# A hybrid decoder block in fp32 on one core: part of the FFN's input as seven half-block products, a wide projection, and a written-out order

## The chip, the cores and the metric

One core of a Trainium2 chip runs the kernel. Its engines work in parallel, each through its own instructions in order: TensorE (PE, matrix products; its weight loads are listed as PEld), VectorE (DVE), ScalarE (ACT), GpSimd (POOL) and SyncE (SP), which here only starts transfers. Transfers are carried out by 16 DMA engines. The metric is the device time of one execution in microseconds; lower is better.

## The reference

One decoder layer on 256 tokens of 1024 channels, all in float32, cut to what matters here:

```
proj = x @ w_in                     # 1024 x 9216: hq hf hi hg | mq mk mv | gate logits
y_a  = hgrn2_mixer(hq, hf, hi) normed, times silu(hg)
y_b  = moba_attention(rope(mq), rope(mk), mv)
g_a, g_b = split(sigmoid(gate_logits + b_gate))
mixed = (g_a * (y_a @ w_branch_a) + g_b * (y_b @ w_branch_b)) @ w_out
x = layer_norm(ALPHA * x + mixed, ln1_w, ln1_b)
h_gate, h_up = split(x @ w_ffn_in)  # 1024 x 2*2816
y = (silu(h_gate) * h_up) @ w_ffn_down
out = layer_norm(ALPHA * x + y, ln2_w, ln2_b)
```

## The kernel before

**Products in split precision.** Each float32 operand is split into a high part, rounded to the format that TensorE takes at full rate, and a low part, the remainder: `split` (L209) casts on ACT and subtracts on DVE. A product is then three: high times high, high times low, low times high. Weights are split on the chip too. `stage` (L217) loads one block of 1 MB into a `raw` buffer (three of them, four once `state["four"]` is set), casts it to `wh` on ACT (L236) and subtracts to `wl` on DVE (L238); there are four `wh` and four `wl` buffers. The blocks come in one fixed list from `plan` (L80), 89 of them. `fetch` (L258) takes the next finished block and first stages more until a given number is ready beyond it (LOOKAHEAD, 3); `prefetch` stages a given number.

**Three ways to arrange a product of 256 columns of weights with 256 tokens.** `feat_pair` (L298): 48 matmuls of 256 columns. `wide_pair` (L306): the high and the low part of the activations lie side by side in a `Pair`, and one matmul of 512 columns multiplies both with `wh`, a second one of 256 columns takes `wl`: 32 matmuls; the two halves of the PSUM bank are added afterwards, with a copy on ACT and an addition on DVE for each 128 columns (`wide_sum`, L321). The third is for 1024 columns of weights: `quad_stage` (L607) makes a 2 x 2 block product (two token halves, two column blocks of 512, two halves of the 1024 input channels) with seven half-block products instead of eight. Each is one `block_product` (L328): 12 matmuls of 512 columns. For that it needs differences of activations (`differences`, L335) and sums of weight blocks.

**Sums of weights.** The sums are made by transfers, not by an engine: `sum_weights` (L247) copies one weight block in DRAM into a tile `u` and adds others onto it with an accumulating transfer, both issued from POOL's queue. Eight transfers (`SUMS`, L46) make the four sums of one product; a blocked pair needs them before its weights are staged. When each is issued is written out: `SUMS_WITH` (L44) names for each of the 32 sums the load behind which it goes. A DVE copy of one element (the tick, L253) and a POOL operation (the mark, L254) tie it there. Sums keep their order in POOL's queue, and a sum that reads or adds to another's result waits there until that one has landed.

**Stages.** Input projection and the scan; gates; value and MoBA products with rope; `za` = y_a @ w_branch_a (wide); `zb` = y_b @ w_branch_b (L769, `feat_pair`); output projection `wo` (L890 to L898) with the first layer norm (`norm1`), whose result is transposed and split into `x1p` (L845); "early" FFN blocks j = 0 and 2, a token half at a time (`FfnEarly`, L855); the FFN loop (L956) over j = 4 to 20 in steps of two: a wide pair `fg` and a wide pair `fu`, silu, product, split into `ah`, `al`; the differences for the down projection (`mixed_a`, L926); the down projection, two 2 x 2 blocks of seven products each (`quad_product`, L986) and six rows of plain products (`rows_pass`); the second layer norm and the store.

**What sets the order.** Outside of `tc.manual_schedule` a planner orders each engine's instructions by a simulated timeline. Inside it, the named engines keep program order. Before the change the first projection, `wo` with the early FFN blocks, and parts of the very end are in such a block; zb, the FFN loop and nearly all of the down projection are the planner's. The residual `xr` (L828) and the norms' weights `wb` (L779, L780) are loaded from POOL's queue.

## Time and profile before

| what | value |
|---|---|
| device time, median of 3 runs | 492.39 us (492.26 to 494.57) |
| span of the profiled execution, first to last instruction | 491.3 us |
| the profiled execution's own time beside the span | not listed; the median stands 1.1 us above the span |
| PE busy | 482.9 us, 98% |
| DVE busy | 396.2 us, 81% |
| ACT busy | 315.6 us, 64% |
| POOL busy | 66.0 us, 13% |
| data moved | 137.79 MB, 280 GB/s |
| zb, starts on PE | from about 259 us |
| wo and early FFN | 283 to 328 us |
| FFN loop | 328 to 429 us |
| down projection and end | 429 to 491 us |

Lines like L315 are lines of the kernel. A row of the timeline gives the start, the length, the engine, line and operation, what it writes and reads, and how often in a row; the time that the engine idled ahead of it stands in brackets. Matmuls overlap: one of 512 columns is listed with 0.39 us, though the next starts sooner. A row of the windows gives for one stretch the busy time of each engine with its count of instructions, the clock that TensorE was granted, the share of time that the DMA engines were busy, and the rate. A row of groups gives the count, the busy time in all, the mean of one in ns, and the idle time ahead.

### The profile page before, as it was taken

How to read it: one execution, taken by the hardware profiler on the slowest of the kernel's cores; microseconds unless marked ns; L12 is line 12 of the kernel's file. 1: busy time of each engine (PE TensorE's matmuls, PEld its weight loads, DVE VectorE, ACT ScalarE, POOL GpSimd, SP SyncE). 2: the span in 40 equal slices, each digit the busy share in tenths (PEclk: the TensorE clock that was granted, in tenths of full speed). 3: DMA queues.
4: the chain of work that ended last, by engine and by line, in shares of the span. 5: the costliest groups of instructions: out<-in, count | busy, mean ns of one | idle time of the engine just before them, and what ended most of it. 6: DMA issues, size and time to landing. Idle time of an engine off the chain costs nothing.

```text
span 491.3 us, 7536 instructions
## 1 busy us (share of the span) xinstructions
PE 482.9 (98%) x2980; PEld 434.0 (88%) x2980; DVE 396.2 (81%) x490; ACT 315.6 (64%) x446; POOL 66.0 (13%) x89
## 2 busy tenths in 40 slices
PE   9999999999999999999999999999999999999994
PEld 9999888888888999999989988888888888898883
DVE  4888899999879869999773999555886779589947
ACT  6797677655879869789762555444565656587700
POOL 2305150530000010010010000001213010000001
PEclk9999999999999999999999999999999999999998
DMA  8879899999996988669776466049999999999702
GB/s 315 371 263 448 273 294 339 316 356 300 343 330 248 318 300 301 229 228 338 255 268 248 177 257 233 18 176 407 286 307 354 317 310 308 297 361 387 257 0 85
DMA packets 25106, 137.79 MB, mean 280 GB/s; under 512 B 2416, under 2 KB 2544, under 8 KB 13424
## 3 DMA queue, kind: packets, MB, share of 16 engines
q1 hardware_dynamic: 15264, 100.63, 53.2%
q0 software_dynamic: 9808, 36.70, 29.0%
q8 instruction: 23, 0.38, 0.3%
q14 instruction: 11, 0.09, 0.0%
HBM read 136.27 MB, written 34.60 MB: 348 GB/s over the span
## 4 chain that ended last, share of the span: by engine, by line
PE 95%; DVE 2%; DMA 2%; issue 0%; ACT 0%; DVEq 0%
PE fu L315 7%; PE fg L315 7%; PE fg L316 3%; PE fu L316 3%; PE gb L315 3%; PE za L315 3%; PE wd L999 2%; PE wd L1000 2%; PE wd L1001 2%; DMA raw<-in_wts_dram 2%; PE sc L514 2%; PE hf L383 2%; PE ga L315 2%; PE hf L384 2%; PE mk L355 2%; PE zb L355 2%
## 5 line engine op out<-in xcount | busy, mean ns | idle before, releaser
L238 DVE TENSOR_TENSOR wl<-raw,wh 128x2048 fp32r<-128x2048 f32 x89 | 203.0, 2289 | 54.0 <-ACT wh L236 53.5
L236 ACT CAST wh<-raw 128x2048 fp32r<-128x2048 f32 x89 | 169.8, 1916 | 73.9 <-PE fg L315 17.6
L315 PE MATMUL fg<-x1p,wh 128*128 128x512 f32 x144 | 50.5, 394 | 0.0
L315 PE MATMUL fu<-x1p,wh 128*128 128x512 f32 x144 | 50.4, 394 | 0.0
L254 POOL TENSOR_TENSOR mark<-ticks 128x1 f32<-128x1 f32 x32 | 24.4, 762 | 180.8 <-DVE ticks L253 159.9
L316 PE MATMUL fg<-x1p,wl 128*128 128x256 f32 x144 | 40.0, 277 | 0.0
L316 PE MATMUL fu<-x1p,wl 128*128 128x256 f32 x144 | 39.9, 277 | 0.0
L315 PEld LDWEIGHTS fu<-x1p,wh 128*128 128x128 f32 x144 | 27.0, 187 | 6.2
L315 PEld LDWEIGHTS fg<-x1p,wh 128*128 128x128 f32 x144 | 27.0, 187 | 6.1
L316 PEld LDWEIGHTS fg<-x1p,wl 128*128 128x128 f32 x144 | 27.0, 188 | 0.1
L316 PEld LDWEIGHTS fu<-x1p,wl 128*128 128x128 f32 x144 | 27.0, 188 | 0.0
L315 PE MATMUL za<-yP,wh 128*128 128x512 f32 x64 | 23.6, 407 | 0.0
L315 PE MATMUL gb<-xP,wh 128*128 128x512 f32 x64 | 22.7, 397 | 0.0
L315 PE MATMUL ga<-xP,wh 128*128 128x512 f32 x64 | 22.6, 396 | 0.0
L256 POOL DMA_DIRECT2D u<-in_wts_dram x24 | 19.7, 827 | 9.7 <-DMA u<-in_wts_dram 7.3
L353 PE MATMUL mq<-xP,wh 128*128 128x256 f32 x64 | 18.6, 291 | 0.0
L354 PE MATMUL mk<-xP,wh 128*128 128x256 f32 x64 | 18.4, 288 | 0.0
L353 PE MATMUL mk<-xP,wh 128*128 128x256 f32 x64 | 18.3, 285 | 0.0
L316 PE MATMUL za<-yP,wl 128*128 128x256 f32 x64 | 18.3, 285 | 0.0
L355 PE MATMUL mq<-xP,wl 128*128 128x256 f32 x64 | 18.2, 284 | 0.0
L355 PE MATMUL mk<-xP,wl 128*128 128x256 f32 x64 | 18.1, 283 | 0.0
L353 PE MATMUL hq<-xP,wh 128*128 128x256 f32 x64 | 18.1, 283 | 0.0
(338 smaller groups left out, 1388.3 us busy)
## 6 DMA issues: line engine op xcount, KB each, us to landing
raw<-in_wts_dram SPq DMA_DIRECT2D x73, 1024.0 KB, 6.3
raw<-u SPq DMA_DIRECT2D x16, 1024.0 KB, 6.7
u<-in_wts_dram POOLq DMA_DIRECT2D x8, 1024.0 KB, 20.5
u<-u POOLq DMA_DIRECT2D x8, 1024.0 KB, 18.2
first<-in_xw_dram SPq DMA_DIRECT2D x6, 640.0 KB, 9.3
xr<-in_x_dram POOLq DMA_DIRECT2D x1, 1024.0 KB, 5.2
wb<-in_ln_w_dram POOLq DMA_DIRECT2D x2, 512.0 KB, 6.6
wb<-in_ln_b_dram POOLq DMA_DIRECT2D x2, 512.0 KB, 7.9
```

The costliest lines, as they stand in the source:

```text
L236: nc.scalar.copy(h[:, ks, :], raw[:, ks, :])
L238: eng.tensor_sub(l[:, ks, :], raw[:, ks, :], r32(h[:, ks, :]))
L254: tc.keep_in_program_order(nc.gpsimd.tensor_tensor(mark, tick, tick, op=ALU.add))
L256: tc.keep_in_program_order(nc.gpsimd.dma_start(source(dst), source(src), **more))
L315: nc.tensor.matmul(ps, wh[:, k, wcol], a.both(k), start=(k == 0), stop=False)
L316: nc.tensor.matmul(ps[:, 0, :], wl[:, k, wcol], a[0, k, slice(0, T)], start=False, stop=(k == KC - 1))
L353: nc.tensor.matmul(ps, wh[:, k, wcol], ah[:, kk, :], start=(kk == 0), stop=False)
L354: nc.tensor.matmul(ps, wh[:, k, wcol], al[:, kk, :], start=False, stop=False)
L355: nc.tensor.matmul(ps, wl[:, k, wcol], ah[:, kk, :], start=False, stop=(kk == KC - 1))
L383: nc.tensor.matmul(pss[f], wh[:, wcol], xTh[:, k, :], start=(k == 0), stop=False)
L384: nc.tensor.matmul(pss[f], wh[:, wcol], xTl[:, k, :], start=False, stop=False)
L514: nc.tensor.matmul(ps[:, a, :], KL[:, h, :], later(Qt, n, h, 1), start=True, stop=True)
```

## The change

Three things, and what they need:

1. The FFN's column blocks j = 4 and 6 (512 gate and 512 up columns: `fg4`, `fu4`, `fg6`, `fu6`, four wide pairs, four loads) leave the loop. They become one `quad_stage` with gate and up columns as its two column blocks: seven products `q0` to `q6`, seven loads, four of them sums of weights. It needs the differences of x1, so a float32 copy of the transposed x1 is kept (`x1Tr`), and eight more sums. Its result lies by tokens, so it is turned by eight transposes (`turned`). `SUMS_WITH` now has 40 entries: the new group's eight go behind loads 29 to 37, and the down projection's sixteen behind loads 38 to 55 (before: four behind 38 to 41, twelve behind 56 to 67, in the FFN loop).
2. zb is made with `wide_pair`; its attention result is a `Pair` now.
3. zb's pairs 1 to 3, the FFN loop and the down projection go into `manual_schedule` for PE, DVE and ACT, with `FFN_ORDER` as the list of steps: `g` and `u` pairs, `q` products, `t` transposes, `m` differences, `s` splits. Each step stages one later load. The splits of most FFN results subtract on POOL instead of DVE. `xr` and `wb1` stand before zb in the program instead of behind it.

```diff
-SUMS_WITH = (2, 3, 4, 5, 6, 7, 8, 10, 9, 11, 12, 13, 14, 15, 16, 26,
-             38, 39, 40, 41, 56, 57, 58, 59, 60, 61, 62, 63, 64, 65, 66, 67)
+SUMS_WITH = (2, 3, 4, 5, 6, 7, 8, 10, 9, 11, 12, 13, 14, 15, 16, 26, 29, 31, 33, 34, 35, 36, 36, 37, 38, 39, 40, 41, 42, 43, 44, 45, 46, 47, 50, 51, 52, 53, 54, 55)
+GROUP = (EARLY * P, FF + EARLY * P)
+FFN_ORDER = [(i[0], int(i[1:])) for i in "g8 u8 g10 q0 u10 q1 g12 q2 u12 q3 g14 q4 u14 q5 m1 g16 t0 q6 u16 g18 t1 m0 s16 u18 s18 g20 u20 s20".split()]
...
-    for j in range(EARLY, NF, 2):
-        add("w_ffn_in", 0, 8, j * P, 256)
-        add("w_ffn_in", 0, 8, FF + j * P, 256)
+    for kind, j in FFN_ORDER:
+        if kind not in "guq":
+            continue
+        if kind == "q":
+            steps.append((quarter("w_ffn_in", 0, GROUP, GATE_PRODUCTS[j]), KQ // 2, False))
+        else:
+            add("w_ffn_in", 0, 8, (FF if kind == "u" else 0) + j * P, 256)
...
-    ybh = slot("ybh", F32R).rearrange("p (h t) -> p h t", h=H)
-    ybl = slot("ybl", F32R).rearrange("p (h t) -> p h t", h=H)
+    yb = Pair("yb")
+    ybh, ybl = Part(yb, 0), Part(yb, 1)
...
+    def zb_pair(j, ordered):
+        z = kept[:, j % 2, :].rearrange("p (f t) -> p f t", f=2)
+        more = stage() if ordered else iter(())
+        wide_sum(wide_pair(f"zb{j}", mm, "mm", yb, 0 if ordered else LOOKAHEAD), [z[:, f, :] for f in range(2)])
+        next(more, None)
+        cs = slice(2 * j, 2 * j + 2)
+        nc.vector.tensor_mul(gb[:, cs, :], z, gb[:, cs, :])
+        nc.vector.tensor_add(ga[:, cs, :], ga[:, cs, :], gb[:, cs, :])
+        next(more, None)
+        split(mTh[:, cs, :], mTl[:, cs, :], ga[:, cs, :])
+        list(more)
...
+        for ks, ps in pss:
+            nc.scalar.copy(x1Tr[:, ks, ts], ps)
...
     with tc.manual_schedule(engines={ET.PE, ET.DVE, ET.Activation}):
+        for j in range(1, 4):
+            zb_pair(j, True)
         tiles = [(2 * q,) + fetch(0) for q in range(4)]
...
+        mixing = differences(lambda t, k: x1Tr[:, k:k + 4, t * P:(t + 1) * P], xs, x1Sh, x1Sl)
         e[1][0].product(0)
+        next(mixing)
         e[1][0].product(1)
         e[0][0].transpose()
         e[0][1].transpose()
+        more = stage()
+        next(more)
         e[1][0].silu()
+        list(more)
+        more = stage()
+        next(more)
         e[1][1].product(0)
         e[1][1].product(1)
...
+        e[1][1].silu()
+        list(more)
+        next(mixing)
+        prefetch(1)
...
+    def late_half(kind, j):
+        i, p, tag = (0, mm, "mm") if kind == "g" and j >= KW else (kind == "u", aux, "aux")
+        pss = wide_pair(f"f{kind}{j}", p, tag, x1p, 0)
+        s = room[:, 2 * i + j // 2 % 2, :, :]
+        for f, ps in enumerate(pss):
+            nc.scalar.copy(s[:, f, :], ps[:, 1, :])
+        more = stage()
+        next(more, None)
+        for f, ps in enumerate(pss):
+            nc.vector.tensor_add(s[:, f, :], ps[:, 0, :], s[:, f, :])
+        both[kind] = s
+        if i == 0:
+            nc.scalar.activation(s, s, AF.Silu)
+            list(more)
+        else:
+            ...
+            nc.vector.tensor_mul(a, both["g"], both["u"])
+            list(more)
+            made[j] = a
+            if j < KW:
+                split_a(j)
...
+        split(ah[i][:, k:k + 2, ts], al[i][:, k:k + 2, ts], made[j][:, :, ts], nc.gpsimd if j >= KQ else nc.vector)
...
+        return quad_stage("gu", Part(x1p, 0), Part(x1p, 1), x1Sh, x1Sl, gu, final, kept[:, 0, :], True, 0)
+
+    def turned(t):
+        ts = slice(t * P, (t + 1) * P)
+        pt = aux.tile([P, 4, P], F32, tag="aux", name=f"gut{t}")
+        for a in range(4):
+            nc.tensor.transpose(pt[:, a, :], gu[:, t, a * P:(a + 1) * P], ident)
+        js = slice(EARLY, EARLY + 4)
+        nc.scalar.copy(araw[0][:, js, ts], pt)
+        split(ah[0][:, js, ts], al[0][:, js, ts], araw[0][:, js, ts], nc.gpsimd)
+
+    products = group()
+    with tc.manual_schedule(engines={ET.PE, ET.DVE, ET.Activation}):
+        for n, (kind, j) in enumerate(FFN_ORDER):
+            state["four"] = n > 0
+            if kind == "q":
+                next(products, None)
+                list(stage())
+            elif kind == "t":
+                turned(j)
+            elif kind == "m":
+                list(mixed_a(j))
+            elif kind == "s":
+                split_a(j)
+            else:
+                late_half(kind, j)
+            if n in (0, 1):
+                e[1][n - 0].transpose()
...
             wh, wl = fetch(0)
...
+            if i == 0:
+                list(stage())
...
+    with tc.manual_schedule(engines={ET.PE, ET.DVE, ET.Activation}):
+        quad_product(0, pss[0][:1])
+        nc.scalar.copy(p, pss[0][0][0])
+        prefetch(1)
+        ...
+        tiles = [(k,) + fetch(0) for k in range(KW, NF, 2)]
+        rows_pass(pss[0], lhs, 0, tiles, NF, True)
+        layer_norm("n2", 0, pss[0], x1[:, 0, :], wb2, x1[:, 0, :], store=out[0:P, :], made=(1,))
         rows_pass(pss[1], lhs, 1, tiles, NF, True)
```

More of the change, by code (lines that the diff above doesn't have):

```diff
@@ L725, in moba_head @@
         nc.tensor.matmul(po[:, P:T], mv[:, 1, hd], pT, start=False, stop=True)
-        split(ybh[:, h, :], ybl[:, h, :], po)
+        split(ybh[:, h, slice(0, T)], ybl[:, h, slice(0, T)], po)
         yield
@@ L766, in hybrid_layer_kernel @@
     gate = pool("gate", 1)
-    mTh = slot("mTh", F32R).rearrange("p (k t) -> p k t", k=KC)
-    mTl = slot("mTl", F32R).rearrange("p (k t) -> p k t", k=KC)
-    for j in range(4):
-        ps = feat_pair(f"zb{j}", ybh, ybl)
-        cs = slice(2 * j, 2 * j + 2)
-        nc.vector.tensor_mul(gb[:, cs, :], ps, gb[:, cs, :])
-        nc.vector.tensor_add(ga[:, cs, :], ga[:, cs, :], gb[:, cs, :])
-        split(mTh[:, cs, :], mTl[:, cs, :], ga[:, cs, :])
     def bcast(name, w, b):
@@ L781, in bcast @@
         return t
+    xr = slot("xr").rearrange("p (t d) -> p t d", t=NT)
+    nc.gpsimd.dma_start(xr, x.rearrange("(t p) d -> p t d", p=P))
+    wb1 = bcast("wb1", ln1_w, ln1_b)
+    mTh = slot("mTh", F32R).rearrange("p (k t) -> p k t", k=KC)
+    mTl = slot("mTl", F32R).rearrange("p (k t) -> p k t", k=KC)
+    kept = gate.tile([P, 2, 512], F32, tag="kept", name="kept")
+    def zb_pair(j, ordered):
[9 more added lines that the diff above has]
+        list(more)
+    for j in range(1):
+        zb_pair(j, False)
     def rows_pass(parts, lhs, t, tiles, ktot, onto=False):
@@ L846, in norm1_transpose @@
         ts = slice(t * P, (t + 1) * P)
+        pss = []
         for g in range(2):
@@ L896, in hybrid_layer_kernel @@
             rows_pass(pss[1], lhs, 1, tiles[q:q + 1], KC)
-            if q < 2:
+            if q == 0:
                 prefetch(1)
-        early = [ready.pop(0) for _ in range(4)]
-        e = [[FfnEarly(t, 2 * i, *early[2 * i:2 * i + 2]) for i in range(2)] for t in range(NT)]
+        more = stage()
+        next(more)
+        early = [ready.pop(0) for _ in range(3)]
+        e = [[None, None], [None, None]]
+        e[0][0] = FfnEarly(0, 0, *early[:2])
         e[0][0].product(0)
@@ L903, in hybrid_layer_kernel @@
         norm1(1)
+        list(more)
+        early.append(ready.pop(0))
+        e[0][1] = FfnEarly(0, 2, *early[2:])
+        e[1] = [FfnEarly(1, 2 * i, *early[2 * i:2 * i + 2]) for i in range(2)]
         e[0][0].silu()
@@ L1030, in hybrid_layer_kernel @@
         rows_pass(pss[1], lhs, 1, tiles, NF, True)
-    with tc.manual_schedule(engines={ET.DVE}):
         layer_norm("n2", 1, pss[1], x1[:, 1, :], wb2, x1[:, 1, :], store=out[P:T, :], made=(0, 1))
```

153 lines of the change are left out of this document (79 added, 74 removed).

## The prediction

> **What bounds the kernel now.** I read the page's first two parts, then what TensorE (PE) waited for, then the windows of the stages that the change touches, and last single rows of the timeline. The page:
>
> ```profile
> span 491.3 us, 7536 instructions
> PE 482.9 (98%) x2980; PEld 434.0 (88%) x2980; DVE 396.2 (81%) x490; ACT 315.6 (64%) x446; POOL 66.0 (13%) x89
> PEclk9999999999999999999999999999999999999998
> ```
>
> PE's waits, both of them, and its last matmul:
>
> ```profile
> PE warm L425 <- PEq L1053: 0.8, 1, 0.8
> PE mv L332 <- DVE wl L238: 0.2, 1, 0.2
> 483.63 0.28 PE L795 MATMUL wd<-wh,al 128*128 128x256 f32 x1
> ```
>
> Between 0.8 and 483.9 us PE waits for 0.2 us, at full clock; the remaining 7.4 us are the last normalisation and the store, which the change leaves alone. So PE's work is the time: each microsecond taken from it is a microsecond, and each wait that the change brings in adds as much. The median of 492.39 stands 1.1 us above this execution's span; I carry that 1.1 us over (its whole time is not listed beside the span).
>
> The stages (columns: length; busy time of PE, weight loads, DVE, ACT, POOL; clock; DMA share; GB/s): value products, rope and scan to 259, zb to 283, output projection and early FFN to 328.4, FFN loop, down projection.
>
> ```profile
> 165.00:193.00 28.00, 28.00 (x191) 25.86 (x190) 22.61 (x21) 21.82 (x50) 3.06 (x3) 1.00 0.88 279
> 193.00:259.00 66.00, 66.00 (x486) 62.64 (x485) 58.12 (x104) 53.67 (x123) 7.23 (x13) 1.00 0.74 274
> 259.00:283.00 24.00, 24.00 (x201) 23.96 (x200) 15.84 (x17) 9.58 (x9) 0.00 (x0) 1.00 0.54 204
> 283.00:328.40 45.40, 45.40 (x212) 37.74 (x211) 34.47 (x41) 21.25 (x22) 2.00 (x2) 1.00 0.48 182
> 328.40:428.80 100.40, 100.40 (x582) 87.82 (x581) 74.88 (x99) 59.52 (x81) 15.74 (x26) 1.00 1.03 314
> ```
>
> DMA is full in the FFN loop (1.03) and has room before it. The second resource to watch is DVE.
>
> **PE's work, part by part.** Busy means overlap, so I take distances between starts.
>
> ```profile
> 190.50 0.39 PE L331 MATMUL mv<-wh,xP 128*128 128x512 f32 x1
> 193.22 0.28 PE L353 MATMUL mk<-xP,wh 128*128 128x256 f32 x1
> 264.01 0.28 PE L353 MATMUL zb<-ybh,wh 128*128 128x256 f32 x1
> 264.13 0.28 PE L354 MATMUL zb<-ybl,wh 128*128 128x256 f32 x1
> 301.68 1.03 PE L851 MATMUL x1t<-ident,x 128*128 128x128 f32 x8
> 302.47 0.48 PE L793 MATMUL wo<-wh,mTh 128*128 128x512 f32 x1
> 345.55 0.39 PE L315 MATMUL fu<-x1p,wh 128*128 128x512 f32 x1
> 351.10 0.39 PE L315 MATMUL fg<-x1p,wh 128*128 128x512 f32 x1
> ```
>
> A wide pair (32 matmuls) takes 351.10 - 345.55 = 5.55 us. One seven-product block (12 matmuls of 512 columns) takes 193.22 - 190.50 = 2.72 us. Eight transposes take 302.47 - 301.68 = 0.79 us. The FFN group (g4, u4, g6, u6) goes from 4 x 5.55 = 22.20 to 7 x 2.72 = 19.04 plus 8 transposes: 2.37 us saved. A zb pair is now 48 matmuls at 264.13 - 264.01 = 0.12, 5.76 us; wide it is 5.55, so four save 0.84. Together **3.2 us**. PE's rate may differ a little in the new mixture; I let the sum run from 2.7 to 3.5.
>
> The Trainium skill, "TensorE: Matmul & The Clock Gate", section "Back-to-back issue gap", gives warm matmuls N/2.4 + 2.5 ns: 216 ns for 512 columns and 109 for 256. By it, an estimate, pairs are 5.20, products 2.59, transposes 56 ns each, and the saving 2.4 us; the rows above (227 and 120 ns) disagree with it, and decide.
>
> **What the other engines get.** The groups by line (count; busy time, mean ns of one; idle time ahead):
>
> ```profile
> L238 DVE TENSOR_TENSOR wl<-raw,wh 128x2048 fp32r<-128x2048 f32 x89 | 203.0, 2289 | 54.0 <-ACT wh L236 53.5
> L236 ACT CAST wh<-raw 128x2048 fp32r<-128x2048 f32 x89 | 169.8, 1916 | 73.9 <-PE fg L315 17.6 <-PE zb L354 14.3 <-DMA raw<-in_wts_dram 13.7
> L966 DVE TENSOR_TENSOR room<-fu,room 128x256 f32<-128x256 f32 x18 | 7.5, 418 | 0.6 <-ACT room L965 0.6
> L623 DVE TENSOR_TENSOR hgs<-hgp,hg 128x512 f32<-128x512 f32 x1 | 0.7, 689 | 0.7 <-PE hg L333 0.7
> L211 DVE TENSOR_TENSOR xSl<-xs,xSh 128x1024 fp32r<-128x1024 f32 x2 | 2.4, 1222 | 0.5 <-ACT xSh L210 0.5
> L372 POOL COPY xTr<-first 128x256 f32<-128x256 f32 x8 | 7.4, 922 | 10.9 <-DMA first<-in_xw_dram 10.8
> ```
>
> In the FFN loop DVE gains three weight subtractions of 2.29 us and eight operations on 128x512 of 0.69 for the products. It loses eight evacuations of 0.42 and two multiplications of 0.69 with the four pairs, and seven splits, which POOL gets (two of 0.42, five of 0.69): 74.9 + 6.9 + 5.5 - 3.4 - 1.4 - 4.3 = 78 of the loop's 97 us. PE's work hides it; uncovered it would cost the 3 us more. ACT gains three casts of 1.92, under the same cover. The wide zb's copies and additions, the copies of x1 that the differences are made from, eight more ticks and eight marks lie on engines with room in their windows (DVE 15.8 of 24, 34.5 of 45.4): nothing. The planner also lays out anew all that stands before zb; no row tells what it will find, and I take nothing. The fixed order removes no wait on PE, since there is none.
>
> The Trainium skill, "SBUF — State Buffer", section "SBUF: two separate sides", says that a GpSimd operation that reads SBUF and a DVE operation with two SBUF inputs lock each other out for a whole instruction. No row shows a POOL subtraction of such a size. By that rule, with the copy of 0.92 us doubled for twice the elements, an estimate, nine splits on POOL could hold DVE up by 17 us in the loop, to 95 of 97: no bound yet, but it speaks for the first rival below.
>
> **The sums.** They run as transfers from POOL's queue.
>
> ```profile
> q1 hardware_dynamic: 15264, 100.63, 53.2%
> q0 software_dynamic: 9808, 36.70, 29.0%
> ```
>
> Of q0's 36.70 MB, 33.6 are the 32 sums: 0.29 x 491.3 x 33.6/36.7 / 32 = 4.1 us of all 16 engines each; a load costs 0.532 x 491.3 / 96 MB-blocks = 2.7. The change adds 8 x 4.1 + 3 x 2.7 = 41 us, and moves 12 sums out of the FFN loop to before it. From 165 to 328.4 the windows leave 3.4 + 17.2 + 11.0 + 23.6 = 55 us free, and 20 more sums want 82. Some 27 us spill into the loop, which has lost 49 and gained 8: it fits there. So the transfers are not a bound as a whole, but POOL's queue lags through the middle of the kernel. Two loads and one normalisation look at that lag.
>
> ```profile
> 178.82 0.33 SPq L233 DMA_DIRECT2D raw<-u  x1
> 188.21 4.49 DVE L238 TENSOR_TENSOR wl<-raw,wh 128x2048 fp32r<-128x2048 f32 x2 [0.83 <-ACT wh L236]
> DMA to landing us min/median/max: 4.8/4.8/4.8
> 219.08 0.33 SPq L233 DMA_DIRECT2D raw<-in_wts_dram  x1
> 221.00 0.54 POOL L256 DMA_DIRECT2D u<-in_wts_dram  x1 [0.25 <-issue]
> DMA to landing us min/median/max: 7.4/7.4/7.4
> ```
>
> The last value product starts at 190.50 and its correction weights are ready at 188.21 + 2.29 = 190.50: no slack. Its load landed in 4.8 us, at 183.6, and then stood until 186.2 for its cast. A load beside a sum took 7.4 us. With sums now behind loads 29, 31 and 33 it lands near 186.2: a wait between 0 and 2 us; I take 0.2, as the slack ahead of the cast is just the difference.
>
> **DVE ahead of the loop.** The differences of x1 (four subtractions of 0.69, two of 1.22: 5.2 us) and one weight subtraction, moved behind the second normalisation, now stand between PE's early FFN blocks and the loop. The loop's third pair needs the first pair's PSUM banks, and DVE works in order. From 328.4, when PE ends the early blocks: activation and product 1.3 us, a weight subtraction 2.3, two differences 1.4, ACT's cast of them 1.0, ACT's next weight cast 1.9, its subtraction 2.3, the first pair's two additions 0.8: 339.4. The third pair wants the banks at 328.4 + 0.3 + 2 x 5.55 = 339.8. A dozen hand-overs lie in between: 0 to 2 us of wait, I take 0.3. After that each step gives DVE 5.55 us for some 3.8 us of work, and it catches up.
>
> The sum: 492.4 - 3.2 + 0.2 + 0.3 = **489.7 us**.
>
> **Rivals.** (1) The loads or DVE take most of it back: the two waits above at their upper ends, 2 + 2, with 3.2 saved, give 493.2; half of them gives 491.2. For it: zero slack in one place, 0.4 us in another. Against: loads beside sums through the whole FFN loop (DMA 1.03) made PE wait nowhere.
>
> (2) Slower: the transfer of x and of the normalisation's weights comes late behind the sums in POOL's queue.
>
> ```profile
> 246.36 0.75 POOL L828 DMA_DIRECT2D xr<-in_x_dram  x1 [9.08 <-PE s L699]
> 292.50 0.68 DVE L804 SCALAR_TENSOR_TENSOR x<-xr,wo 128x512 f32<-128x512 f32 x1
> 295.57 1.41 DVE L812 SCALAR_TENSOR_TENSOR x<-x,n1a,wb 128x512 f32<-128x512 f32 x2
> 296.89 1.41 DVE L815 SCALAR_TENSOR_TENSOR x<-x,n1a,wb 128x512 f32<-128x512 f32 x2
> ```
>
> They are issued at 246.4 and wanted at 292.5 and 295.6; the normalisation ends at 298.3, and PE's transposes stand at 301.68, so 3.4 us of delay cost nothing. If the sums of loads 29 to 42 go first, nine more than now, that is 37 us; 20.6 are free by 259, 11 more by 283, and the rest is through at about 293: no wait. If loads 43 and 44 go first too, 8.2 us more at 0.52 free make it 309: 13 late, 10 us of wait, 499.7. It decides from 300 on. The same queue holds the scan's powers of the RMS norm (L556), which would wait behind a sum that waits for another to land.
>
> (3) The order written out for the FFN and down projection makes PE wait once per step, where the planner had found an order without a wait: 21 steps of the loop and 14 of the down projection at 0.2 us are 7 us, 496.
>
> (4) No effect: the saving is eaten to within 0.7 us, 492. For it only that (1) can take any size.
>
> **How the numbers follow.** The bound for "no change" is 0.5%, 2.46 us, about what a measurement of this kernel can tell: 489.93 to 494.85. Forecast, with waits up to 0.7 us: 0.47, its own range 488.8 to 489.9, all of it faster. (1) and (4): 0.34, same. (2): 0.13, of which 0.09 above 494.85. (3): 0.06, of which 0.05 above. So faster 0.47, same 0.39, slower 0.14. The range reaches from the best sum without waits (492.4 - 3.5 = 488.9, and 0.3 for the spread of medians) to the middle of (2) and (3): 488.6 to 496.
>
> **What would show it.** PE's products in the loop 2.72 us apart and zb pairs 5.55: the saving is right. PE's list of waits: empty but for the start, forecast; a wait of a value product for DVE's weights near 190 or of the third pair for DVE near 340, (1); DVE's normalisation waiting for xr or wb, and PE's transposes for it, (2); many waits of 0.1 to 0.5 us in the loop, (3). A PE that idles over 1 us between 0.8 us and its last matmul makes the forecast wrong, and so would a tail other than 7.4 us.

## The result, and the profile after

The change makes the kernel slower: 497.88 us (median of 6 runs, 497.47 to 501.82) beside 492.42 us of the kernel before on the same chip, a ratio of 1.0123 (95% interval 1.0103 to 1.0143), some 5.5 us. The forecast was 489.7, its range ended at 496.

In the runs further down, one execution each of `early_mix`, `mix_pool` and `zb_part` (its profiled one) was disturbed and far longer; the medians in us still count it, the ratios leave it out.

The profiled execution took 497.47 us, its span is 495.7, 4.4 us more than before. Of the rest of the 5.5, 0.4 is that this was the shortest of the six. The other 0.6 is that the profiled execution before was longer than its median: 222 executions of that kernel beside the later runs list time and span, and the time is 1.7 to 1.8 us above the span in each, so a span of 491.3 stands for some 493.0 us (an estimate; its own time is not listed). The page after, its first part and its transfers:

```profile
span 495.7 us, 7392 instructions
PE 482.6 (97%) x2880; PEld 426.7 (86%) x2880; DVE 411.3 (83%) x504; ACT 326.5 (66%) x459; POOL 97.3 (20%) x114
DMA  8879999899997999899999999999999647499802
```

PE has 100 instructions fewer and is busy for 0.3 us less, and it now waits. Its list of waits (in all, how often, the longest), which held one entry of 0.2 us beside the start:

```profile
PE wd L818 <- DVE wl L245: 2.0, 2, 1.2
PE fe L895 <- DVE x1p L218: 1.0, 1, 1.0
PE mk L362 <- DVE wl L245: 0.9, 1, 0.9
...
PE mv L339 <- DVE wl L245: 0.4, 1, 0.4
```

Where the 4.4 us lie is read from the first matmuls of the stages. Timeline of PE before, then after:

```profile
258.99 0.28 PE L353 MATMUL zb<-ybh,wh 128*128 128x256 f32 x1
282.61 0.40 PE L793 MATMUL wo<-wh,mTh 128*128 128x512 f32 x1
328.44 0.39 PE L315 MATMUL fg<-x1p,wh 128*128 128x512 f32 x1
428.75 0.39 PE L999 MATMUL wd<-wh,ah 128*128 128x512 f32 x1
```

```profile
260.47 0.39 PE L322 MATMUL zb<-yb,wh 128*128 128x512 f32 x1
283.26 0.40 PE L817 MATMUL wo<-wh,mTh 128*128 128x512 f32 x1
330.32 0.39 PE L322 MATMUL fg<-x1p,wh 128*128 128x512 f32 x1
347.62 0.40 PE L338 MATMUL gu<-wh,x1p 128*128 128x512 f32 x1
350.37 0.39 PE L322 MATMUL fu<-x1p,wh 128*128 128x512 f32 x1
356.00 0.40 PE L338 MATMUL gu<-wh,x1Sh 128*128 128x512 f32 x1
429.80 0.40 PE L1104 MATMUL wd<-wh,ah 128*128 128x512 f32 x1
488.15 0.28 PE L819 MATMUL wd<-wh,al 128*128 128x256 f32 x1
```

| stretch | before | after | difference |
|---|---|---|---|
| up to zb | 258.99 | 260.47 | +1.48 |
| zb | 23.62 | 22.79 | -0.83 |
| output projection, early FFN | 45.83 | 47.06 | +1.23 |
| FFN loop | 100.31 | 99.48 | -0.83 |
| down projection, to the start of its last matmul | 54.88 | 58.35 | +3.47 |
| from there to the end | 7.67 | 7.55 | -0.12 |

The loop gives 0.83 in place of 2.37: a product takes 350.37 - 347.62 = 2.75 us, as thought, but a wide pair 356.00 - 350.37 = 5.63, not 5.55, although no wait stands in it. The largest loss is in the down projection, whose products the change leaves as they were. What precedes it, as windows of the last 10 us of the loop (before, then after; the last two columns are the DMA's share and GB/s):

```profile
420.00:430.00 10.00, 10.00 (x58) 8.70 (x57) 6.84 (x8) 5.25 (x7) 1.13 (x2) 1.00 1.01 313
```

```profile
420.00:430.00 10.00, 10.00 (x58) 8.68 (x57) 9.30 (x12) 7.55 (x12) 2.85 (x4) 1.00 0.33 126
```

DVE is full (9.30 of 10) and the DMA idles. The reason stands in the timelines of DVE, ACT and POOL after, in the written order of step `m0` and of the evacuation and weight cast behind it:

```profile
419.17 1.78 DVE L984 TENSOR_TENSOR kept<-araw 128x512 f32<-128x512 f32 x1
420.88 0.68 DVE L985 TENSOR_TENSOR kept<-araw 128x512 f32<-128x512 f32 x1
...
420.99 0.62 ACT L217 CAST ah<-kept 128x512 fp32r<-128x512 f32 x1 [2.14 <-DVE kept L984]
423.57 1.35 ACT L217 CAST sb<-kept 128x512 fp32r<-128x512 f32 x2 [1.36 <-DVE kept L989]
425.34 0.64 ACT L1014 COPY room<-fu 128x256 f32<-128x256 f32 x2
425.87 1.93 ACT L243 CAST wh<-raw 128x2048 fp32r<-128x2048 f32 x1
...
418.93 1.48 POOL L218 TENSOR_TENSOR al<-araw,ah 128x512 fp32r<-128x512 f32 x1 [10.36 <-ACT ah L217]
```

The pair `fu18` had ended at 418.5, its bank is read at 425.34. All four raw buffers were full, so for 11 us no load was asked for. Two issues that follow each other:

```profile
419.28 0.32 SPq L240 DMA_DIRECT2D raw<-u_w_ffn_down  x1
430.15 0.32 SPq L240 DMA_DIRECT2D raw<-u_w_ffn_down  x1
```

Loads that are asked for late come to the down projection late. Its products want one each 2.72 us. A load of that stretch lands 7 to 8 us after its issue and frees its buffer some 4.3 us after that, so four buffers give one each 2.9 us, and the issues are in fact 3.0 us apart. Four matmuls start late for it, at 460.61, 469.18, 472.07 and 474.51. With the slower matmul behind each they cost 3.3 of the 3.47 us, of which the list of waits counts 2.0:

```profile
472.07 0.50 PE L818 MATMUL wd<-wl,ah 128*128 128x512 f32 x1 [1.22 <-DVE wl L245]
474.51 0.50 PE L818 MATMUL wd<-wl,ah 128*128 128x512 f32 x1 [0.77 <-DVE wl L245]
```

The transfers issued from 425 to 476 us (KB each, median us to landing):

```profile
raw<-u_w_ffn_down SPq DMA_DIRECT2D x5, 1024.0 KB, 7.4
```

This was my reading before the runs below.

### The profile page after: what moved, and what is told of

Its sections match the earlier page's. It is cut to its first block, busy times and chain, and to the rows that moved or that the text cites. A ratio compares the mean times of both kernels' runs of the same rounds, so it can differ in the third digit from the quotient of the medians.

```text
span 495.7 us, 7392 instructions
## 1 busy us (share of the span) xinstructions
PE 482.6 (97%) x2880; PEld 426.7 (86%) x2880; DVE 411.3 (83%) x504; ACT 326.5 (66%) x459; POOL 97.3 (20%) x114
## 5 line engine op out<-in xcount | busy, mean ns | idle before, releaser
L245 DVE TENSOR_TENSOR wl<-raw,wh 128x2048 fp32r<-128x2048 f32 x92 | 210.5, 2294 | 45.0 <-ACT wh L243 44.7
L261 POOL TENSOR_TENSOR mark<-ticks 128x1 f32<-128x1 f32 x40 | 35.5, 887 | 144.8 <-DVE ticks L260 144.7
L322 PE MATMUL fg<-x1p,wh 128*128 128x512 f32 x112 | 39.9, 399 | 0.0
L322 PE MATMUL fu<-x1p,wh 128*128 128x512 f32 x112 | 39.9, 399 | 0.0
L323 PE MATMUL fg<-x1p,wl 128*128 128x256 f32 x112 | 31.4, 281 | 0.0
L323 PE MATMUL fu<-x1p,wl 128*128 128x256 f32 x112 | 31.4, 281 | 0.0
L322 PEld LDWEIGHTS fg<-x1p,wh 128*128 128x128 f32 x112 | 21.0, 188 | 5.1
L322 PEld LDWEIGHTS fu<-x1p,wh 128*128 128x128 f32 x112 | 21.0, 188 | 5.0
L218 POOL TENSOR_TENSOR al<-araw,ah 128x512 fp32r<-128x512 f32 (+1 forms) x6 | 13.2, 2195 | 55.6 <-ACT ah L217 55.6
L322 PE MATMUL zb<-yb,wh 128*128 128x512 f32 x64 | 22.3, 394 | 0.0
L360 PE MATMUL mk<-xP,wh 128*128 128x256 f32 x64 | 18.4, 287 | 0.0
```

The lines of the kernel that those rows point to most:

```text
L218: eng.tensor_sub(dst_l, src, r32(dst_h))
L245: eng.tensor_sub(l[:, ks, :], raw[:, ks, :], r32(h[:, ks, :]))
L261: tc.keep_in_program_order(nc.gpsimd.tensor_tensor(mark, tick, tick, op=ALU.add))
L322: nc.tensor.matmul(ps, wh[:, k, wcol], a.both(k), start=(k == 0), stop=False)
L323: nc.tensor.matmul(ps[:, 0, :], wl[:, k, wcol], a[0, k, slice(0, T)], start=False, stop=(k == KC - 1))
L360: nc.tensor.matmul(ps, wh[:, k, wcol], ah[:, kk, :], start=(kk == 0), stop=False)
```

## The experiments

One table for all runs. Ratio: to the kernel before, in runs on the same chip. Stretches in us, from first matmul to first matmul in one profiled execution each: gates to `za` (gb-za), zb, output projection and early FFN (wo-fg), loop, down projection to the start of its last matmul.

| run | us | ratio (95%) | gb-za | zb | wo-fg | loop | down |
|---|---|---|---|---|---|---|---|
| before | 492.42 | 1 | 155.90 | 23.62 | 45.83 | 100.31 | 54.88 |
| after | 497.88 | 1.0123 (1.0103 to 1.0143) | 157.96 | 22.79 | 47.06 | 99.48 | 58.35 |
| zb_alone | 497.92 | 1.0087 (1.0063 to 1.0111) | 155.39 | 23.20 | 50.23 | 100.31 | 54.88 |
| zb_ordered | 494.82 | 1.0025 (1.0007 to 1.0043) | 157.18 | 23.20 | 47.59 | 100.31 | 54.88 |
| zb_full | 494.05 | 1.0021 (1.0008 to 1.0033) | 157.48 | 23.20 | 45.83 | 102.09 | 54.88 |
| zb_part | 492.83 | 0.9980 (0.9967 to 0.9994) | | | | | |
| zb_part_again | 493.10 | 0.9987 (0.9971 to 1.0003) | 155.46 | 23.20 | 45.83 | 100.31 | 54.88 |
| no_down_sums | 497.38 | 1.0083 (1.0061 to 1.0106) | 157.98 | 22.79 | 45.81 | 99.47 | 58.20 |
| no_sums | 495.69 | 1.0053 (1.0033 to 1.0074) | 156.80 | 22.79 | 45.82 | 99.47 | 58.72 |
| sums_moved | 499.41 | 1.0137 (1.0087 to 1.0187) | 158.40 | 22.78 | 45.84 | 101.25 | 63.17 |
| sums_gap | 496.26 | 1.0072 (1.0055 to 1.0089) | 157.74 | 22.78 | 45.84 | 99.47 | 57.96 |
| early_mix | 498.49 | 1.0104 (1.0063 to 1.0146) | 156.98 | 24.37 | 47.14 | 99.50 | 58.50 |
| mix_mid | 499.28 | 1.0125 (1.0099 to 1.0151) | 157.68 | 22.79 | 46.86 | 103.41 | 56.25 |
| mix_and_sums | 502.56 | 1.0188 (1.0161 to 1.0216) | 157.17 | 22.78 | 45.84 | 103.70 | 61.75 |
| no_mix | 494.97 | 1.0052 (1.0019 to 1.0085) | 162.10 | 24.28 | 47.05 | 99.47 | 54.92 |
| mix_pool | 500.14 | 1.0137 (1.0121 to 1.0152) | 155.54 | 24.73 | 46.99 | 99.47 | 61.20 |
| splits_dve | 498.73 | 1.0095 (1.0070 to 1.0121) | 158.90 | 22.79 | 47.27 | 99.47 | 59.43 |
| free_ffn | 502.18 | 1.0179 (1.0117 to 1.0240) | 161.29 | 23.12 | 47.26 | 103.06 | 57.50 |
| free_both | 501.60 | 1.0154 (1.0113 to 1.0195) | 161.38 | 24.44 | 46.97 | 103.25 | 55.77 |
| pair_entry | 501.34 | 1.0158 (1.0130 to 1.0187) | 158.14 | 23.89 | 47.01 | 102.05 | 58.16 |

Some expectations count the down projection to the end of its last matmul, 0.28 us more.

### The weight sums

`no_down_sums` leaves the down projection's sixteen sums out, `no_sums` the FFN group's eight as well; their loads take unsummed blocks.

```diff
-    sums = ... + summed(("w_ffn_in", 0, GROUP)) + summed(*(("w_ffn_down", k, 0) for k in range(0, KW, KQ)))
+    sums = ... + summed(("w_ffn_in", 0, GROUP))          # no_down_sums; in no_sums this one goes too
```

> The changed kernel without the 16 weight sums of the down projection: these five products of each half load an unsummed block instead, so the output of the down projection is not the reference's; all loads and products stay in number and size. 16 x 4.1 = 66 us of DMA time go, all of them between 190 and 330 us. Theory 1 (the sums delay the loads of the values and early FFN stages, the order delays those of the down projection): the waits at 186 to 191 and at 306 us go, 1.5 to 2.5 us, and the 3.5 us of the down projection stay: 495.4 to 496.4 us. Rival (one cause: transfers late everywhere): all of 5.5 us go, 492.4 us. Second rival (the sums cost nothing, DVE alone is late): 497.9.

> The changed kernel without the 24 weight sums of the FFN group and of the down projection (the loads take unsummed blocks, so the output is not the reference's). This bounds what the sums cost where they stand: theory, the values stage starts its output projection at 230.4 us as in the kernel before, no wait at 306 us, the down projection still 3.5 us longer: span 493 or a little below. Rival: the values stage is late without them too (the wide MoBA pairs or the order make it so): 495.

What the sums do to a load beside them is seen in the transfers issued between 242 and 260 us (KB each, median us from issue to landing), after and in `no_down_sums`:

```profile
raw<-in_wts_dram SPq DMA_DIRECT2D x3, 1024.0 KB, 18.4
```

```profile
raw<-in_wts_dram SPq DMA_DIRECT2D x3, 1024.0 KB, 7.1
```

Loads 45 to 47 land after 18.4 us in place of 7.1. Their lateness runs on through the staging to the normed rows' split at 306 us: with sums there the wo-fg stretch takes 46.9 to 47.3 us in all nine forms of the changed kernel that have them, without them 45.8 in all five (these two, `sums_moved`, `sums_gap`, `mix_and_sums`). So the 1.23 us belong to the sums' place. In five of the same nine zb is longer too, by 1.1 to 1.9 us; in `no_mix` it waits for a split that stands on DVE behind the subtraction of load 45, which had landed after 21.7 us. The loop does not care (99.47 with and without), and the down projection loses as much as with the sums: there theory 1 holds, and the rival of one cause falls. By the ratios `no_down_sums` gave back some 2.0 us (1.0123 to 1.0083), which is within theory 1's 1.5 to 2.5, but not where it said: the wait at 306 us went, and the stretch before `za` kept its length (157.98 and 157.96). `no_sums` gave back some 3.4 us; its span of 494.5 lies nearer to the rival's 495 than to the 493 of its theory.

The stretch before `za` can't be settled so. In the six executions without any added sum it takes 155.4 to 157.5 us (median 156.4), in the eleven with the group's sums behind loads 29 to 37 from 155.5 to 162.1 (median 158.0). The sums seem to lengthen it by 1 to 2 us, and single executions differ by more: the three of 161 us and over hold one wait of PE of 1.8 to 3.3 us and 3.4 us at half the clock behind it.

`sums_moved` and `sums_gap` ask for the same sums elsewhere:

```diff
-SUMS_WITH = (..., 29, 31, 33, 34, 35, 36, 36, 37, 38, 39, 40, 41, 42, 43, 44, 45, 46, 47, 50, 51, 52, 53, 54, 55)
+SUMS_WITH = (..., 36, 37, 38, 39, 40, 41, 42, 43, 49, 50, 51, 52, 53, 54, 55, 56, 57, 58, 59, 60, 61, 62, 63, 64)  # sums_moved
+SUMS_WITH = (..., 29, 31, 33, 34, 35, 36, 36, 37, 38, 39, 40, 41, 42, 43, 51, 52, 53, 54, 55, 56, 57, 58, 59, 60)  # sums_gap
```

> The changed kernel with its 24 later weight sums asked for elsewhere: the FFN group's eight behind loads 36 to 43 (there before: 29 to 37), the down projection's sixteen behind loads 49 to 64 (there before: 38 to 55). In the changed kernel loads 31 to 37 and 45 to 52 landed 7 to 19 us after their issue, without the down projection's sums 5 to 8. Theory: the loads of the zero-slack places then land in 5 to 7 us, and the waits of the values stage, the wide MoBA pairs and the early FFN go, 2 to 3 us: 492.5 to 493.5 of span. Rival: the sums meet the FFN's loads instead and the loop or the down projection grows by as much: 495 or more.

> The changed kernel with the down projection's sums asked for behind loads 38 to 43 and 51 to 60 in place of 38 to 47 and 50 to 55, so that fewer of them meet loads 44 to 50 and none has to wait until 413 us, as two did with the sums behind loads 49 to 64. Theory: the wait at 306 us goes or halves (1.25 us), and the FFN loop and down projection stay as they are: span 494.4 to 495. Rival: the last sums are late for the down projection's summed blocks and the stage grows by more: 496 and up.

Later is worse: in `sums_moved` the last two sums went out at 413.7 and 427.1 us and the second of them stood ahead of five splits in POOL's queue; the down projection took 63.2. With the gap alone the wait at 306 is gone, the other stretches stay within 0.4 us, and the time is 496.26, the best with all of the change in it. The theory for `sums_gap` holds; its span of 494.2 is a little below the 494.4 to 495 expected.

### The differences and the written order

`no_mix` leaves the two halves' differences out (the mixed products take a plain block). The others keep all of the work: `early_mix` moves it a little within the written order, `mix_mid` does it in the middle of the loop, `mix_and_sums` with `sums_moved` beside it; `mix_pool` puts the differences' eight low-part subtractions on POOL; `splits_dve` takes the loop's nine splits back to DVE; `free_ffn` and `free_both` write the order out for PE alone.

```diff
-... g14 q4 u14 q5 m1 g16 t0 q6 u16 g18 t1 m0 s16 u18 s18 g20 u20 s20
+... g14 q4 u14 q5 g16 t0 q6 u16 g18 t1 s16 u18 s18 g20 u20 s20                             # no_mix
+g8 u8 q0 g10 q1 u10 q2 g12 q3 u12 q4 g14 q5 u14 q6 m1 g16 t0 m1 t1 u16 m0 s16 g18 m0 u18 s18 g20 u20 s20   # early_mix
+g8 u8 q0 q1 g10 q2 q3 u10 q4 q5 g12 q6 t0 u12 t1 m0 g14 m0 u14 m1 g16 m1 u16 s16 g18 u18 s18 g20 u20 s20   # mix_mid
...
-            split(difference(n, m, 0), difference(n, m, 1), s[:, m])
+            split(difference(n, m, 0), difference(n, m, 1), s[:, m], nc.gpsimd)             # mix_pool
...
-    with tc.manual_schedule(engines={ET.PE, ET.DVE, ET.Activation}):
+    with tc.manual_schedule(engines={ET.PE}):                                               # free_ffn
```

> The changed kernel with one edit: the fixed order of the FFN. The seven half-block products stand from the second wide pair on, the second half's differences after the last of them in two halves with a wide pair between, and the first half's differences likewise, two wide pairs earlier than in the changed kernel. Theory 1: the down projection lost its 3.5 us because 6 us of differences stand in DVE's and ACT's order ahead of the evacuation of a pair and of the weight staging behind it, so that raw buffers stay full, the DMA idles between 380 and 430 us and the loads then come too late. It gives back 2 to 3.5 us: 494.5 to 496 us. Rival: the loads between 430 and 470 are bound by the DMA whatever the order is (7.3 us to land), and the time stays at 497.9.

> The changed kernel without the differences of the two halves of the activations (eight subtractions, eight splits; the down projection's mixed products take the plain block in their place, so its output is not the reference's). Instructions of TensorE, loads and sums are those of the changed kernel. Theory 1 (12 us of differences in DVE's and ACT's order hold up the staging ahead of the down projection): the stage takes 55 to 56 us, the span is 492.5 to 493.5. Rival (the loads of 430 to 470 us are bound by their own cycle): 58 us, 495.5.

> The changed kernel with the FFN's order rewritten so that the differences are done early: the seven products two by two between the first wide pairs, the first half's differences around the gate pair of block 14, the second half's around the gate pair of block 16, and five wide pairs behind them before the down projection. Without any differences the down projection took 55.2 us in place of 58.6, so DVE's and ACT's lateness at the end of the loop is the cause. Theory: with five pairs to make it good (each leaves DVE 1.5 us and more) the stage takes 55 to 56 us and the span falls by 2.5 to 3.5 us, to 492.5 to 493. Rival: the lateness is not made good (as with the differences only two pairs earlier: 58.8), and the span stays at 495 to 496.

> Both edits above. If the two causes are separate, their gains add: 5 to 6 us off the changed kernel's span, 490 us, and 491.5 for the time, level with or below the kernel before. Rival: with the products early in the loop and the sums in it, the two meet, and no more than one of the gains is left: 493.

> The changed kernel with the eight low-part subtractions of the two halves' differences on POOL in place of DVE: 5.5 us less for DVE in the last third of the FFN loop, some 14 us more for POOL. Leaving out all of the differences (12 us of DVE) brought the down projection from 58.6 to 55.2 us, putting nine splits on DVE (6 us) took it to 59.7. Theory: DVE's lateness is the cause, and the stage takes 56.5 to 57.5 us, the span 494 to 494.7. Rival: DVE and ACT wait for POOL's slower subtractions in the written order, and the stage stays at 58.6 or grows.

> The changed kernel with the nine activation splits of the FFN loop subtracted on DVE instead of POOL. On POOL they took 1.3 to 2.9 us each, on DVE 0.65. Theory 1 (DVE's fixed order is what is late in the loop and at its end): DVE gets 6 us more work and the time rises by 1 to 3 us, to 499 to 501. Rival (POOL's subtractions hold up DVE's, as the Trainium skill has it in its page on memories): DVE's others get shorter by as much and the time falls by 0 to 2 us, 496 to 498.

> The changed kernel with the FFN loop's order written out for TensorE alone; DVE and ACT take their work in the scheduler's order, as in the kernel before. Moving the differences within the written order gave nothing back (58.8 us for the down projection and what follows, 58.35 in the changed kernel, 54.9 before). Theory 1: the written order itself costs the lead, since DVE and ACT wait for each other at every stage; the down projection takes 55 to 56.5 us and the span is 492.5 to 494. Rival: DVE has too much to do at the end of the loop in any order; the stage stays at 58 to 59 us and the span at 495.7.

> As the one above, with the down projection's order too written out for TensorE alone. If it is the order of the down projection that keeps its loads late, this gives another 1 to 2 us beside the run above; if the lead is lost ahead of it, both have the same span.

The window of the whole loop, after and in `no_mix`, and the down projection of `no_mix`:

```profile
330.32:429.80 99.48, 99.48 (x546) 85.71 (x545) 81.08 (x81) 63.69 (x80) 17.31 (x12) 1.00 0.82 271
```

```profile
336.08:435.55 99.47, 99.47 (x545) 85.69 (x544) 73.58 (x69) 61.38 (x74) 20.93 (x13) 1.00 0.85 287
...
435.55 0.40 PE L1104 MATMUL wd<-wh,ah 128*128 128x512 f32 x1
490.47 0.28 PE L819 MATMUL wd<-wh,al 128*128 128x256 f32 x1
```

With 7.5 us less for DVE in the loop the down projection takes 490.47 - 435.55 = 54.92 us: all 3.4 are back, and the ratio is 1.0052 in place of 1.0123. (The profiled execution of `no_mix` was one of its longer ones, 499.78 us beside a median of 494.97; the surplus lies before `za`.) So the loss comes from DVE's and ACT's work in the loop. The rival, that the loads' own cycle sets the stage, falls with it, and the loads land sooner here. The transfers issued from 425 to 476 us in `no_mix`, to be held against the 7.4 above:

```profile
raw<-u_w_ffn_down SPq DMA_DIRECT2D x5, 1024.0 KB, 4.8
```

Behind the gap of the changed kernel the DMA is full (a share of 0.95 to 1.00 from 430 to 454 us, where `no_mix` has 0.63 up to 446) and each load takes longer; why it then moves 351 GB/s from 446 to 454 us, and in `no_mix` 395, is not shown.

None of the orders tried gave the loss back. Loop and down projection together take 155.2 us before, 157.8 after, 154.4 in `no_mix`, and with all the work in another order 158.0 (`early_mix`), 159.7 (`mix_mid`), 160.6 (`free_ffn`), 159.0 (`free_both`). In `mix_mid` the down projection did fall to 56.3, as hoped, but now PE waited in the loop, for the products' results to be turned:

```profile
PE gut L1065 <- DVE gu L1057: 2.0, 1, 2.0
PE fg L322 <- ACT araw L1067: 0.9, 1, 0.9
```

Whether the place or the amount of the work decides is open. `early_mix` does not test the place, though it was written to: it moves half of `m0` one wide pair ahead, and the other half comes later, so that the last difference (DVE's last subtraction of `m0`) starts 4.3 us before the down projection, where it was 6.2 in the changed kernel. The kernel before makes the same differences in its loop, but spread out, the last one 20.9 us ahead. By and large the down projection is the shorter, the longer that lead:

| run | last difference starts ahead of the down projection, us | down, us |
|---|---|---|
| mix_pool | 3.6 | 61.20 |
| early_mix | 4.3 | 58.50 |
| splits_dve | 5.9 | 59.43 |
| after | 6.2 | 58.35 |
| free_ffn | 9.2 | 57.50 |
| free_both | 9.2 | 55.77 |
| mix_mid | 16.5 | 56.25 |
| before | 20.9 | 54.88 |

This speaks for the place and does not show it: the three with a lead of 9 to 17 us and all of the work paid 3.6 to 3.9 us in the loop, each with a wait of PE of 2.0 us for the turning of the products' results and 3.4 us at half the clock behind it, and while PE is late the loads gain time. (That loss makes both sides of `free_ffn`'s expectation fail.) An order with the differences early and the turning not waited for was not tried. Nor is it DVE's time alone: `mix_pool` frees DVE of eight subtractions, and its down projection grows to 61.2. POOL takes 1.3 us for each where DVE took 0.69; DVE waits twice for it, 1.5 us each, and two of its subtractions beside POOL's take 1.76 and 1.77 us in place of 0.68. Which of these costs the time was not separated. `mix_and_sums` has both losses, and both sides of its expectation fail.

`splits_dve` gives DVE nine splits, and the down projection is 1.1 us longer; the interval of its ratio overlaps that of the changed kernel, so these runs cannot tell whether the splits on POOL gain or lose.

### The entry of a wide pair

The spacing of matmuls in the loop is of two kinds. From one 512-wide matmul of a pair to the next it is 350 and 343 ns by turns, 346.7 in the mean, or 361, 349 and 350 in turn, 353.3 in the mean; a pair of 32 matmuls is 5.55 us or 5.64 to 5.66. The kind changes only where something else stands between. `pair_entry` puts two transposes of the identity ahead of each wide FFN pair.

```diff
+            if f == 0 and name[0] == "f":
+                for u in range(2):
+                    nc.tensor.transpose(ps[:, 0, u * P:(u + 1) * P], ident, ident)
```

> The changed kernel with two transposes of the identity (0.07 us each) into each wide FFN pair's own bank ahead of its first matmul, which overwrites them. In all traces a wide pair's spacing is of one of two kinds, 346.7 ns for a 512-wide and a 256-wide matmul each time, or 360.7 ns each third time; the kind changes only where other work or a wait stands between, and every pair behind a product was of the slow kind. Theory: the entry decides, and with transposes ahead some or all pairs run at 5.55 us: the loop then takes 99.0 to 100.2 us in place of 99.47 with 14 x 0.14 us of transposes in it. Rival: something of the loop (its buffers' places, the other engines' traffic) decides; all pairs stay at 5.64 and the loop takes 101.4.

Seven of the 14 pairs now ran at the faster spacing almost throughout, where in the changed kernel all behind a product were of the slow kind; that what stands ahead of a pair changes its kind is shown, the gain is not: the transposes and the slower first matmul behind them cost more, and the loop took 102.05, outside of what either side expected. In `mix_mid` all seven pairs behind the wait above took 5.55 us as well. The next experiments show the same from the other side.

### The MoBA projection alone

The kernel before with zb wide and nothing else of the change (`zb_alone`); with its last three pairs in the written order and the residual's loads ahead (`zb_ordered`); with the change's places of staging up to the loop (`zb_full`); with these up to the second norm only (`zb_part`).

```diff
-        ps = feat_pair(f"zb{j}", ybh, ybl)
+        for f, ps in enumerate(wide_pair(f"zb{j}", mm, "mm", yb)):                     # zb_alone
...
-        prefetch(2)
-        norm1(0)
+        prefetch(1)
+        norm1(0)
+        prefetch(1)                                                                    # zb_full, zb_part
...
```

> The kernel before with one part of the change alone: MoBA's projection in wide pairs; no group, no added sums, no fixed order. My term for this part is 4 x (5.76 - 5.55) = 0.84 us, and the trace of the changed kernel showed 23.64 -> 22.79 us for this stage. If the parts add, the time is 491.5 us (0.998 of before) and the four pairs take 22.8 us. Rival: a later wait (the residual rows, the ends of the DVE's norm) takes it back, and the time is 492.4.

> The kernel before with the MoBA projection wide and its last three pairs in the written order of the change, the residual rows' loads ahead of it as there. Wide alone, in the scheduler's order, cost 3.5 us of span: the last pair's difference went to DVE behind weight subtractions, and the output projection waited 1.9 and 1.7 us for it. Theory: in the written order these waits are gone, as in the changed kernel, and the span is 490.5 (0.85 less than before). Rival: in this surrounding the output projection still waits, and the span is 492 or more.

> The kernel before with the MoBA projection wide and ordered as in the change, and now also the change's own places of the weight staging in the output projection, the first layer norm and the early FFN; FFN loop and down projection as before. With the pairs ordered but the staging left where it was, a wait of 1.5 us stood at 306 us, since two weight subtractions then came ahead of the normed rows' split on DVE; in four variants of the changed kernel without sums between 243 and 305 us this stretch took 26.75 us, as before. Theory: no such wait, the 0.85 us are kept, 490.5 us of span and a ratio of 0.998. Rival: a wait of the same size stands elsewhere, and the ratio is 1.000 to 1.003.

> As the last form of the kernel before with the MoBA projection wide, but with the change's staging only up to the second layer norm; from the second row tile's transposes on the staging stands as before. In that last form the wait at 306 us was gone, but the FFN loop took 102.1 us in place of 100.3: its wide pairs ran at 5.64 us, since the transposes of the early blocks had moved from behind the 4th and 45th matmul of the loop to the 12th and 48th. Here they stand at 4 and 45 again. Theory (the entry decides a pair's rate): the loop is back at 100.3 us, the MoBA projection takes 23.2 in place of 23.6 us, no wait at 306: 490.9 us of span, ratio 0.997 to 1.000. Rival: the loop stays at 102 us, the rate having another cause: ratio 1.002 to 1.003.

> The same kernel again, since the profiled execution of the run above had TensorE's clock at 0.56 and shows no spacing. Theory: wide pairs of the FFN at 346.7 ns each, loop 100.3 us, MoBA projection 23.2 us, span 490 to 491. Rival: pairs of the slow kind, loop 102 us.

Three times the saving was lost at another place. PE's waits in `zb_alone`, in the scheduler's order:

```profile
PE wo L799 <- DVE mTl L211: 1.7, 1, 1.7
PE wo L797 <- ACT mTh L210: 1.5, 1, 1.5
```

In `zb_ordered`:

```profile
PE fe L878 <- DVE x1p L211: 1.3, 1, 1.3
PE mk L355 <- DVE wl L238: 1.0, 1, 1.0
```

In `zb_full` the wait of 1.3 is gone (one of 0.8 for `mk` stays, at 153 us), and the loop is 1.78 us longer without a wait in it:

```profile
328.89 0.39 PE L315 MATMUL fg<-x1p,wh 128*128 128x512 f32 x1
430.98 0.40 PE L1023 MATMUL wd<-wh,ah 128*128 128x512 f32 x1
```

The transposes of the early blocks had moved by 8 and 3 matmuls, and 16 of the loop's 18 pairs entered the slow kind. `zb_part` puts these transposes back, and with them the staging behind the second norm. The page is that of `zb_part_again`, the same kernel run a second time:

```profile
span 490.5 us, 7421 instructions
...
258.68 0.40 PE L315 MATMUL zb<-yb,wh 128*128 128x512 f32 x1
281.88 0.40 PE L806 MATMUL wo<-wh,mTh 128*128 128x512 f32 x1
327.70 0.39 PE L315 MATMUL fg<-x1p,wh 128*128 128x512 f32 x1
428.02 0.39 PE L1018 MATMUL wd<-wh,ah 128*128 128x512 f32 x1
```

The loop is back at 100.32 us, nothing waits, and with 0.9980 (0.9967 to 0.9994) and 0.9987 (0.9971 to 1.0003) this is the one form that is level with or a little faster than the kernel before. zb itself takes 23.20 us there, since its pairs are of the slow kind: 0.42 of the 0.84 us.

## Why the prediction was wrong, step by step

**PE's work is the time.** Right: the six stretches' differences, with PE's waits and spacing, make up the whole 4.4 us, and the end is as long as before (7.55 and 7.67). The 1.1 us outside of the span was too little (1.7 to 1.8, as said above), which changes nothing in the forecast difference. The prediction's own sign of being wrong came: PE idled 4.8 us in all by its list of waits between 0.8 us and its last matmul, where it allowed 1.

**zb saves 0.84.** Right in the changed kernel (0.83).

**The FFN group saves 2.37.** The step that failed here is "a wide pair takes 5.55 us", taken from the old loop, where pairs follow each other, for a loop in which products stand between them: 14 x 0.09 = 1.3 us are lost, and 7 x 0.03 on the products; 2.37 - 1.3 - 0.2 = 0.9, measured 0.83. The allowance of 2.7 to 3.5 us for the rate was too narrow; both savings together were 1.66.

**DVE's extra work is covered: "PE's work hides it; uncovered it would cost the 3 us more".** This is the failed step that turned the sign: cover was taken for granted, and PE waited for DVE's weight blocks. The sum was near (78 us expected, 81.1 measured, of 99.5). That the price, 3.47 us, is near the "3 us" is luck: those were the microseconds that DVE got on top, and what PE lost was set by how late the loads were when the down projection began. Wrong was to judge cover by the busy share of the whole loop. In its last 10 us DVE was busy for 9.3, ACT waited for it and it for ACT, and the loads behind them stopped. None of the rivals had this: no sentence named what follows the loop, a stage with one load each 2.72 us and no room to catch up.

**POOL's splits.** The Trainium skill ("SBUF — State Buffer", section "SBUF: two separate sides") has a GpSimd operation that reads SBUF and a DVE operation with two SBUF inputs lock each other out for a whole instruction. The trace agrees: the DVE subtraction at 419.17 above began beside a POOL split and took 1.78 us, its twin 0.68. But the 17 us of delay for DVE that the prediction allowed for did not come. The nine splits took 18.7 us on POOL, and DVE's instructions beside them, each against the shortest of its kind, were stretched by 2.2 us in all. That 18.7 is near 17 is luck, as it holds POOL's own waiting: a split of 128x512 with no DVE work beside it took 1.30 us (`mix_pool`, at 399.04), and those beside a weight subtraction up to 2.89. So here it was mostly POOL that waited. Putting the splits back changed nothing that can be told.

**The sums: "it fits there".** Right for the volume (the loop's DMA share is 0.82), wrong for latency. I looked at two loads and one normalisation. Those were harmless: xr and wb made nothing wait, so rival (2) is wrong as the estimate of 293 us said. Loads 45 to 47 were not on my list, and their 18.4 us cost 1.23 us at 306 and, in some executions, 1.1 to 1.9 in zb.

**The load at 190.50, "0 to 2, I take 0.2".** PE's wait there was 0.4, and 0.9 up to 153.6, where programs with the old sums wait 0.8 to 1.0 too (`zb_ordered`, `zb_full`). What of the 1.48 us up to zb is the sums' doing, and what the planner's, which the prediction took as nothing because no row told of it, stays open; in other executions of the same stretch it was up to 6.

**The third pair, 0.3.** No wait stands in PE's list at 340.

**Rivals.** (1) named the right kind of wait, of PE for DVE behind late loads, with a ceiling of 4 us that held for its two places only. (3), a wait in each step of the written order, is wrong: 99.47 us in seven runs leave no room for one, and with DVE's and ACT's order left to the planner (`free_ffn`) the loop was 3.6 us longer. But the written order is also what put the last differences 6.2 us ahead of the down projection, where the planner had them 20.9 ahead; what part of the 3.47 us that is, stays open. (4) is wrong.

## What to carry to other kernels

An engine that is idle for a fifth of a loop is no cover for more work if it must be on time at the loop's end: ask what the next stage demands per load, and how many loads it has in hand when it starts. A duration read from a row holds for the neighbours that it had there; where the mixture of instructions changes, bound the rate by the widest spread that the same shape shows anywhere in the trace. For a transfer that is added, look at the landing time of every load beside it, not at the sum of bytes.

## What had not been expected of the hardware

The two kinds of spacing: the same 512-wide and 256-wide matmuls on the same buffers take 346.7 or 353.3 ns in the mean, and keep to it for up to 263 pairs of matmuls. A first distance of 340 ns was followed by the slower kind, 443 by the faster, but 430 and 431 by either, so what about the entry decides is open. It is worth 1.8 us of a 100 us loop (`zb_full`) and changes with the place of the early blocks' transposes.

A wait of about 2 us cost more than itself here, since TensorE's clock fell behind it. In `mix_mid`, behind waits of 2.0 and 0.9 us (windows: length, busy times, clock, DMA's share, GB/s), and in `no_mix`, behind one of 1.9 us at 203 us:

```profile
386.00:388.00 2.00, 0.86 (x5) 0.62 (x6) 0.90 (x2) 1.97 (x3) 0.00 (x0) 0.85 1.05 442
388.00:390.00 2.00, 2.00 (x7) 1.71 (x8) 2.00 (x3) 2.00 (x4) 1.53 (x1) 0.50 0.54 225
390.00:392.00 2.00, 2.00 (x11) 1.72 (x10) 1.97 (x3) 1.43 (x3) 0.73 (x1) 0.79 0.58 164
```

```profile
205.60:207.60 2.00, 1.96 (x12) 1.92 (x12) 2.00 (x1) 2.00 (x10) 0.00 (x0) 0.70 0.72 283
207.60:209.60 2.00, 1.40 (x8) 1.20 (x7) 2.00 (x8) 1.96 (x3) 1.16 (x2) 0.50 0.92 283
```

In `mix_mid` the clock's missing share is 0.30 + 1.00 + 0.42 = 1.7 us, a part of it while PE stood still. All six waits of 1.9 us or more in these runs were followed by some 3.4 us at 0.50. Of three of 1.8 us one was (`free_both`, from 197.3 to 200.7) and two were not (`pair_entry` at 205.5, `sums_moved` at 477.9, both at 1.00 behind); none of the shorter ones was. The Trainium skill, "TensorE: Matmul & The Clock Gate", section "What's actually happening", has the clock halved after an idle window of about 3.4 us; in these runs waits of PE shorter than that were enough.

A split of 128x512 on POOL took 1.8 to 2.3 us in the mean; a subtraction of that shape on DVE takes 0.68. Without DVE work beside it the split took 1.30, as said above. The groups of POOL after (count; busy, mean ns):

```profile
L218 POOL TENSOR_TENSOR al<-araw,ah 128x512 fp32r<-128x512 f32 x4 | 9.0, 2252 | 50.1 <-ACT ah L217 50.1
L218 POOL TENSOR_TENSOR al<-room,ah 128x512 fp32r<-128x512 f32 x3 | 5.5, 1836 | 13.9 <-ACT ah L217 13.9
```
